# A hybrid decoder trunk on one core: the order of the first loads, the queue of the depthwise taps, and VectorE's convolution chunks in halves of tokens

## The chip, the core and the metric

The program runs on one core of one Trainium2 chip. The core has five engines with a queue of instructions each: TensorE (PE in the profile, its weight loads PEld), VectorE (DVE), ScalarE (ACT), GpSimd (POOL) and SyncE (SP, which here only issues DMAs). An engine runs its own queue strictly in order and waits for semaphores of the others. The metric is the device time of one execution in microseconds. Lower is better.

## What is computed

A two-layer trunk is run on 512 prompt tokens and on 32 sample tokens (8 sequences of 4). Layer 0 is a conformer convolution module, layer 1 stick-breaking attention; each is followed by a convolutional feed-forward block. The change lies in layer 0's first part:

```python
def conformer_conv(h, past, w_in, b_in, w_dw, b_dw, ln_g, ln_b, w_out, b_out):
    u = h @ w_in + b_in                      # h = rms_norm(x); 1024 -> 2048
    a, gate = jnp.split(u, 2, axis=-1)
    glu = a * jax.nn.sigmoid(gate)
    ext = jnp.concatenate([past, glu], axis=1)
    y = causal_dwconv(ext, w_dw, b_dw)       # 31 taps in each of 1024 channels
    y = jax.nn.silu(layer_norm(y, ln_g, ln_b))
    return y @ w_out + b_out, ext[:, -(CONV_WIDTH - 1):]
```

Everything is float32 in and out.

## The kernel before

**Layout and products.** Activations lie transposed: 128 channels on the partitions, eight chunks of channels, 544 tokens along the row (512 of the prompt, then 32). The tokens are worked in two halves, SA (256 tokens) and SB (256 and the 32 samples, so 288). A float32 product is made from three matmuls of a rounded high part and a rest: weights come as `raw` tiles (1 MB, two column chunks of 128, two buffers); ACT casts each column chunk to `whi` (L327), DVE takes the rest `wlo` (L330); such a pair is a slot, and five are kept. In the same way the activations lie as XH and XL. One product of a slot with one token half is 24 matmuls (L650 to L652) into one of four `acc` banks of PSUM.

**The start** (L579 to L619). SP's queue issues, in this order: `mrow` (norm gains), the first two x blocks, the first two weight tiles in column halves (`Ring.load`, L293), the other x blocks and the sample tokens `xs`, eight small loads for `trow` (the first half of the tap rows for TensorE's chunks), two `scr` loads (the convolution's state). GpSimd's queue issues the biases into `mrow`, the seven loads of `prow` (taps and other parameters as rows), some memsets, and the other half of `trow`. Source order and issue order differ for `scr` and `trow`: the profile has `scr` first.

**A list made ahead** (class `Plan`, L77). All work of layer 0 is entered as operations with an engine, an assumed duration, and what they read and write. `run` (L156) plays this list through and fixes each engine's order for PE, DVE, ACT and POOL: it takes the operation that can start first, less a small bonus for the length of what hangs on it, less `urgent`. On the chip each engine then keeps this order whatever the real durations are. `ARRIVE` (L58) holds the assumed times at which loads land. SP's queue is not part of this order; a load goes out when what its buffer waits for is done and what is ahead in the queue has been issued.

**Operations around the change.**
- `WARM` (L915): matmuls without use that keep TensorE busy before data arrive.
- `incoming(h)` (L868): x is transposed on TensorE (L878, into banks `tr` and `av`), ACT scales it to XH (L885), DVE makes XL (L887), one of both copies xT (L891, L893); ACT squares (L896), and from these `rstd` is made (L900 to L912) as a row for all partitions, by a matmul with `dg` (L909).
- `conv_in` (L923): products of four slots with one half; `glu` (L678) evacuates them: `va` (L687) and `sg` (L683) on DVE, both multiplied by `rstd`, the sigmoid on ACT (L685), the product into `ext_p` (L689).
- The depthwise convolution: chunks 2 to 7 go to TensorE (`conv_tensor`, L767) by 32 x 32 diagonal tap matrices `wdg`, which GpSimd makes from `tapc` and `eye` (L763), from copies `rep` of the rows, shifted by a round trip through memory (`shifted`, L739). Chunks 0 and 1 go to DVE (`conv_vector`, L720): for each, one ACT operation for the first tap and 30 SCALAR_TENSOR_TENSOR of 512 columns (L729, L732), accumulating in `dwa`.
- `param_cols` (L855) turns `mrow` and `prow` into columns `prm`; `turn_taps` (L936) turns `trow`, from which ACT copies `tapc` (L942).
- `conv_sample` (L702): the same convolution for the sample tokens on DVE (L711, L716, L718).
- `add_sum` (L785) adds the chunks to `ysum` (L793); `layer_norm(0)` begins with a matmul of it (L809), then subtracts the mean on DVE (L817), and so on.

Of the kernel before, what the change touches and what calls it, by code (L numbers as in the profile page):

```python
# [17 lines left out]
P = 128  # L18
# [23 lines left out]
REPB = 4  # L42
X_AFTER = 2
MORE = 3
# [27 lines left out]

BIG = 1.0e17
E_BUFS, S_BUFS, W_BUFS = 3, 2, 3

# [122 lines left out]
def tile_trunk(  # L198
# [84 lines left out]
    class Ring:  # L283
# [9 lines left out]
        def load(self):  # L293
            if self.nraw >= len(raws):
                return
            src, nk = raws[self.nraw]
            t = ring.tile([P, NC, 2 * P], F32, tag="raw", name=f"raw{self.nraw}", bufs=RAW_BUFS)
            if self.nraw < RAW_BUFS:
                for half in range(2):
                    cols = slice(half * P, (half + 1) * P)  # L300
                    nc.sync.dma_start(out=t[:, :nk, cols], in_=src[:, :, cols])
            else:
                nc.sync.dma_start(out=t[:, :nk, :], in_=src)
            self.raw[self.nraw] = t
            self.nraw += 1

        def prep(self, later=None):
# [60 lines left out]
    def pcol(row, c):  # L368
        return prm[:, c, row:row + 1]
# [18 lines left out]
    def uid(s):  # L388
        _n[0] += 1
        return f"{s}_{_n[0]}"  # L390
# [9 lines left out]
    def act_table(name):  # L400
        tc.keep_in_program_order(act.preload_act_table_set(name))
# [208 lines left out]
    pool.memset(ext_p[:, :, PAST + SEQ:], 0.0)  # L610
    for i, q in enumerate((nc.sync, pool)):
        ch0 = (PE_CHUNKS[0] + i * len(PE_CHUNKS) // 2) * P
        for m in range(8):
            nj = min(4, CW - 4 * m)
            q.dma_start(out=trow[i][m * n_g:(m + 1) * n_g, :nj * 32].rearrange("g (j h) -> g j h", j=nj),
                        in_=conv_w_dw[0, 4 * m:4 * m + nj, ch0:ch0 + n_g * 32].rearrange("j (g h) -> g j h", h=32))
    scf = state_conv.rearrange("o b t d -> (o b t) d")
    for i in range(2):
        nc.sync.dma_start(out=scr[i], in_=scf[i * 120:(i + 1) * 120, :])  # L619

# [41 lines left out]
    def prepare(slot, begin, place):  # L662

        low = []
        raw = slot // 2
        plan.op("act", 0.95, lambda: begin(low), r=[("raw", slot)], w=[*place, ("slot", slot), "prep"])
        plan.op("dve", 1.135, lambda: low[0](), r=[("raw", slot)], w=[("slot", slot), "low"])
        if slot % 2:
            plan.op(f"raw{raw}", 4.5, lambda: None, w=[("raw", slot + 2 * RAW_BUFS + i) for i in (-1, 0)], r=[("slot", slot)])

# [3 lines left out]
    def ext(c, *parts):  # L674

        return [("ext", c, i) for i in parts or range(4)]
# [42 lines left out]

    def conv_vector(c):  # L720

        acc = buf("ctmp", "dwa", [P, SEQ], 2)
        for k in range(CW):
            src = ext_p[:, c, k:k + SEQ]
            if k == 0:
                plan.op("act", 0.6, lambda src=src: act.activation(
                    acc(), src, AF.Identity, scale=pcol(0, c), bias=pcol(R_BDW, c)), r=[*ext(c), "prm"], w=[acc])
            elif k < CW - 1:
                plan.op("dve", 0.61, lambda k=k, src=src: dve.scalar_tensor_tensor(  # L729
                    acc(), src, pcol(k, c), acc(), op0=ALU.mult, op1=ALU.add), r=[*ext(c), "prm"], w=[acc])  # L730
            else:
                plan.op("dve", 0.61, lambda k=k, src=src: dve.scalar_tensor_tensor(  # L732
                    yc[:, c, 0:SEQ], src, pcol(k, c), acc(), op0=ALU.mult, op1=ALU.add),
                    r=[acc, "prm"], w=[("y", c, 0), ("y", c, 1)] + ext(c))

# [118 lines left out]

    def param_cols(rows_t, n, col, r, w):  # L855
# [6 lines left out]
        plan.op("pe", 0.85, turn, r=[r], w=[pt], urgent=URGENT)  # L862
# [3 lines left out]
    param_cols(mrow, 4, R_MIX, "mrow", "mix")  # L866

    def incoming(h):  # L868
# [26 lines left out]
        for t, m, b in mine:  # L895
            plan.op("act", 1.05, lambda t=t, m=m, b=b: act.activation(  # L896
                junk[:m, :D], t, AF.Square, accum_out=ssq[:m, b:b + 1]), r=[("x", b)], w=["junk", ("ss", b)])
        for lo, hi, m in ([(0, 2, P)], [(2, 4, P), (4, 5, NS)])[h]:
# [15 lines left out]

    warm = psum("acc")  # L915
    for i in range(WARM):
        plan.op("pe", 0.1, lambda: pe.transpose(warm()[:, :P], ident, ident), w=[warm])
    incoming(0)
# [16 lines left out]

# [28 lines left out]
    def settle():  # L964
# [1334 lines left out]
```

## Time and profile before

| | us |
|---|---|
| median of 3 runs (lowest, highest) | 1320.45 (1320.37, 1322.04) |
| the profiled execution, its time | 1320.71 |
| its span in the trace | 1319.0 |
| TensorE busy | 1292.6 |
| VectorE busy | 979.0 |
| ScalarE busy | 679.0 |
| GpSimd busy | 161.4 |

A line of a timeline or chain has the start in us, the busy time, the engine, the source line, the operation, output and inputs, the shape and a count; in square brackets stands how long the engine sat idle before it and what ended that. A count above one merges instructions that follow one another; the steps between them are then less than the length of one, because instructions overlap at their ends. A table of stretches gives the busy time of each engine between two times, the mean granted clock of TensorE and the busy share of the DMA engines. Times are from the start of the span.

### The profile page before, as it was taken

How to read it: one execution, taken by the hardware profiler on the slowest of the kernel's cores; microseconds unless marked ns; L12 is line 12 of the kernel's file. 1: busy time of each engine (PE TensorE's matmuls, PEld its weight loads, DVE VectorE, ACT ScalarE, POOL GpSimd, SP SyncE). 2: the span in 40 equal slices, each digit the busy share in tenths (PEclk: the TensorE clock that was granted, in tenths of full speed). 3: DMA queues.
4: the chain of work that ended last, by engine and by line, in shares of the span. 5: the costliest groups of instructions: out<-in, count | busy, mean ns of one | idle time of the engine just before them, and what ended most of it. 6: DMA issues, size and time to landing. Idle time of an engine off the chain costs nothing. (4 is left out here: it accounts for less than half of the span.)

```text
span 1319.0 us, 26810 instructions
## 1 busy us (share of the span) xinstructions
PE 1292.6 (98%) x11066; PEld 1229.5 (93%) x11066; DVE 979.0 (74%) x1651; ACT 679.0 (51%) x1242; POOL 161.4 (12%) x291
## 2 busy tenths in 40 slices
PE   8999999999999999999999999999999999999997
PEld 7997789999999999999999877789999999999996
DVE  4599786788996886868334588875997996886863
ACT  5521385545554454445323688863655555454452
POOL 3200014111010010000122113210011010010000
PEclk9899999999999999999999999999999999999998
DMA  8263443022333233144456224431223233233221
GB/s 233 65 168 116 113 129 99 30 90 88 97 114 112 65 114 113 57 138 146 163 170 191 92 83 137 129 125 65 80 66 112 97 114 110 67 113 97 73 74 68
DMA packets 124492, 142.40 MB, mean 108 GB/s; under 512 B 5672, under 2 KB 117992, under 8 KB 124099
## 3 DMA queue, kind: packets, MB, share of 16 engines
q1 hardware_dynamic: 118003, 122.43, 29.3%
q0 software_dynamic: 6080, 18.25, 4.5%
q8 instruction: 87, 1.43, 0.5%
q14 instruction: 34, 0.28, 0.1%
q10 hardware_dynamic: 288, 0.02, 0.0%
HBM read 129.34 MB, written 12.18 MB: 107 GB/s over the span
## 5 line engine op out<-in xcount | busy, mean ns | idle before, releaser
L327 ACT CAST whi<-raw 128x1024 fp32r<-128x1024 f32 (+2 forms) x244 | 223.1, 917 | 164.1 <-PE tr L1251 31.6
L330 DVE TENSOR_TENSOR wlo<-raw,whi 128x1024 fp32r<-128x1024 f32 (+2 forms) x244 | 256.3, 1055 | 67.1 <-ACT whi L327 66.6
L650 PE MATMUL acc<-XH,whi 128*128 128x288 f32 (+1 forms) x384 | 115.9, 302 | 0.0
L652 PE MATMUL acc<-XH,wlo 128*128 128x288 f32 (+1 forms) x384 | 112.4, 293 | 1.8 <-DVE wlo L330 1.8
L651 PE MATMUL acc<-XL,whi 128*128 128x288 f32 (+1 forms) x384 | 112.5, 293 | 0.0
L414 PE MATMUL acc<-XH,whi 128*128 128x288 f32 (+1 forms) x360 | 107.8, 299 | 1.1 <-DVE xT L2254 1.1
L416 PE MATMUL acc<-XH,wlo 128*128 128x288 f32 (+1 forms) x360 | 103.9, 289 | 0.5 <-DVE wlo L330 0.5
L415 PE MATMUL acc<-XL,whi 128*128 128x288 f32 (+1 forms) x360 | 104.0, 289 | 0.0
L1450 PE MATMUL acc<-TH,whi 128*128 128x272 f32 x288 | 82.9, 288 | 0.0
L1452 PE MATMUL acc<-TH,wlo 128*128 128x272 f32 x288 | 82.9, 288 | 0.0
L1451 PE MATMUL acc<-TL,whi 128*128 128x272 f32 x288 | 82.8, 287 | 0.0
L1486 ACT COPY G<-acc 128x272 f32<-128x272 f32 (+1 forms) x72 | 26.8, 373 | 105.3 <-PE acc L1452 90.5
L650 PEld LDWEIGHTS acc<-XH,whi 128*128 128x128 f32 x384 | 73.7, 192 | 2.7 <-issue 2.1
L652 PEld LDWEIGHTS acc<-XH,wlo 128*128 128x128 f32 x384 | 74.0, 193 | 2.2 <-DVE wlo L330 2.2
L1251 PE MATMUL av<-HL,whi 128*128 128x288 f32 (+1 forms) x256 | 74.6, 291 | 0.3 <-DVE HL L1504 0.3
L1252 PE MATMUL av<-HH,wlo 128*128 128x288 f32 (+1 forms) x256 | 74.1, 289 | 0.7 <-DVE wlo L330 0.7
L1250 PE MATMUL av<-HH,whi 128*128 128x288 f32 (+1 forms) x256 | 74.5, 291 | 0.0
L651 PEld LDWEIGHTS acc<-XL,whi 128*128 128x128 f32 x384 | 73.9, 192 | 0.5
L1250 PE MATMUL tr<-HH,whi 128*128 128x256 f32 (+1 forms) x256 | 73.4, 287 | 0.0
L1251 PE MATMUL tr<-HL,whi 128*128 128x256 f32 (+1 forms) x256 | 73.3, 286 | 0.0
L1252 PE MATMUL tr<-HH,wlo 128*128 128x256 f32 (+1 forms) x256 | 73.0, 285 | 0.0
L414 PEld LDWEIGHTS acc<-XH,whi 128*128 128x128 f32 x360 | 67.8, 188 | 3.9 <-issue 2.4
(395 smaller groups left out, 4307.3 us busy)
## 6 DMA issues: line engine op xcount, KB each, us to landing
raw<-in_ffn_w_gate_dram SPq DMA_DIRECT2D x22, 1024.0 KB
raw<-in_ffn_w_up_dram SPq DMA_DIRECT2D x22, 1024.0 KB
raw<-in_ffn_w_down_dram SPq DMA_DIRECT2D x24, 768.0 KB
raw<-in_attn_w_qkv_dram SPq DMA_DIRECT2D x12, 1024.0 KB
raw<-in_conv_w_in_dram SPq DMA_DIRECT2D x6, 1024.0 KB
rep<-glu SPq DMA_DIRECT2D x36, 142.0 KB
raw<-in_conv_w_out_dram SPq DMA_DIRECT2D x4, 1024.0 KB
raw<-in_ffn_w_down_dram SPq DMA_DIRECT2D x8, 512.0 KB
```

The lines of the kernel that those rows point to most:

```text
L327: act.copy(hi[:, :n, :], src)
L330: dve.tensor_tensor(lo[:, :n, :], src, hi[:, :n, :], op=ALU.subtract)
L414: pe.matmul(o, hi[:, k, :], xh[:, k, c0:c0 + n], start=(k == 0), stop=False)
L415: pe.matmul(o, hi[:, k, :], xl[:, k, c0:c0 + n], start=False, stop=False)
L416: pe.matmul(o, lo[:, k, :], xh[:, k, c0:c0 + n], start=False, stop=(k == nk - 1))
L650: pe.matmul(o, hi[:, k, :], XH[:, k, c0:c0 + n], start=(k == 0), stop=False)
L651: pe.matmul(o, hi[:, k, :], XL[:, k, c0:c0 + n], start=False, stop=False)
L652: pe.matmul(o, lo[:, k, :], XH[:, k, c0:c0 + n], start=False, stop=(k == NC - 1))
L1250: pe.matmul(o, hi[:, j + k, :], xh, start=(start and k == 0), stop=False, **kw)
L1251: pe.matmul(o, hi[:, j + k, :], xl, start=False, stop=False, **kw)
L1252: pe.matmul(o, lo[:, j + k, :], xh, start=False, stop=(stop and k == len(xs) - 1), **kw)
L1450: pe.matmul(o, hi[:, j + k, :], xh, start=(start and k == 0), stop=False, **kw)
```

## The change

Six things are altered, all in layer 0's beginning:

1. SP issues the first loads in another order: `mrow`, x blocks 0 and 1, the two halves of the first weight tile, the first half of the second, x blocks 2 and 3, the second half, the sample tokens. The biases go out on ACT's queue.
2. All 16 `trow` loads go out on GpSimd's queue. The `scr` loads are entered in the list, behind slot 3.
3. The warm matmuls are bf16, 256 columns of a zeroed tile, 45 instead of 40, and do not wait for `ident`.
4. The squares of the first two x blocks are on DVE instead of ACT; the columns of `prow` are made before `incoming(1)` is entered.
5. DVE's chunks 0 and 1 are convolved in halves of 256 tokens: 120 SCALAR_TENSOR_TENSOR of 256 columns and four ACT operations, instead of 60 of 512 and two. The first halves are entered behind `conv_in(0, 0)`, with `dwa` in another pool, so that they need not wait for the start's buffers to be freed.
6. The assumed landing times, the raw tiles' 4.5 to 5.1, and the tap's assumed 0.61 to 0.345 for half the columns.

```diff
-WARM = 40
+WARM = (17, 28)
+WARM_URGENT = 2.5
...
-ARRIVE = {"mrow": 3.2, ("x", 0): 4.4, ("x", 1): 5.9, ("raw", 0): 7.3, ("raw", 1): 8.8, ("raw", 2): 10.3, ("raw", 3): 11.9,
-          ("x", 2): 13.5, ("x", 3): 15.0, ("x", 4): 15.4, "prow": 18.0, "trow": 24.0, "scr": 19.0}
+ARRIVE = {"zero": 1.2, "mrow": 4.8, ("x", 0): 5.0, ("x", 1): 6.6, ("raw", 0): 9.0, ("raw", 1): 10.8, ("raw", 2): 12.6,
+          "prow": 12.0, ("x", 2): 14.4, ("x", 3): 16.2, ("raw", 3): 18.0, ("x", 4): 18.4, "trow": 20.0}
...
+VTAP = 0.345
...
+        def half(self, i):
+
+            src, nk = raws[self.nraw]
+            if not i:
+                self.raw[self.nraw] = ring.tile([P, NC, 2 * P], F32, tag="raw", name=f"raw{self.nraw}", bufs=RAW_BUFS)
+            cols = slice(i * P, (i + 1) * P)
+            nc.sync.dma_start(out=self.raw[self.nraw][:, :nk, cols], in_=src[:, :, cols])
+            self.nraw += i
...
+    zero = conv.tile([P, 2 * P], BF16, name="zero")
+    dve.memset(zero, 0.0)
+    act.dma_start(out=mrow[2:4, :], in_=conv_b_in.rearrange("o (t d) -> (o t) d", t=2))
     act_table("sqrt_and_others")
     nc.sync.dma_start(out=mrow[0:2, :], in_=norm_mix)
     for b in range(2):
         nc.sync.dma_start(out=xr[b], in_=x_prompt[0, b * P:(b + 1) * P, :])
-    for _ in range(X_AFTER):
-        W.load()
+    for i in (0, 1, 0):
+        W.half(i)
     for b in range(2, 4):
         nc.sync.dma_start(out=xr[b], in_=x_prompt[0, b * P:(b + 1) * P, :])
+    W.half(1)
     nc.sync.dma_start(out=xs, in_=x_sample.flatten_outer_dims())
-    for _ in range(RAW_BUFS - X_AFTER):
-        W.load()
-    pool.dma_start(out=mrow[2:4, :], in_=conv_b_in.rearrange("o (t d) -> (o t) d", t=2))
...
-    for i, q in enumerate((nc.sync, pool)):
+    for i in range(2):
...
-            q.dma_start(out=trow[i][m * n_g:(m + 1) * n_g, :nj * 32].rearrange("g (j h) -> g j h", j=nj),
+            pool.dma_start(out=trow[i][m * n_g:(m + 1) * n_g, :nj * 32].rearrange("g (j h) -> g j h", j=nj),
...
-    def conv_vector(c):
+    def conv_vector(c, h):
-        acc = buf("ctmp", "dwa", [P, SEQ], 2)
+        acc = buf(conv, "dwa", [P, 256], 2)
+        lo = 256 * h
+        keys = ext(c, 1, 2, 3) if h else ext(c, 0, 1)
         for k in range(CW):
-            src = ext_p[:, c, k:k + SEQ]
+            src = ext_p[:, c, lo + k:lo + k + 256]
...
+    plan.op("sp", 11.0, states, r=[("slot", 3)], w=["scr"])
...
+            else:
+                plan.op("dve", 1.2, lambda t=t, m=m, b=b: dve.scalar_tensor_tensor(
+                    junk[:m, :D], t, 1.0, t, op0=ALU.mult, op1=ALU.mult, accum_out=ssq[:m, b:b + 1]),
+                    r=[("x", b)], w=["junk", ("ss", b)])
...
+        pe.matmul(warm[0][:, :2 * P], zero[:, :P], zero, start=True, stop=True)
...
+    param_cols(prow, R_MIX, 0, "prow", "prm")
     incoming(1)
     table("sigmoid_and_others")
-    param_cols(prow, R_MIX, 0, "prow", "prm")
...
     conv_in(0, 0)
+    for c in (0, 1):
+        conv_vector(c, 0)
     late["op"] = plan.op("none", 0.0, settle, w=["mrow", "prow", "trow", "scr"] +
                          [(k, b) for b in range(5) for k in ("x", "ss", "dg")])
     conv_in(0, 1)
     for c in (0, 1):
-        conv_vector(c)
+        conv_vector(c, 1)
         conv_sample(c)
```

More of the change, by code (lines that the diff above doesn't have):

```diff
@@ L42 @@
 REPB = 4
-X_AFTER = 2
 MORE = 3
@@ L297, in load @@
             t = ring.tile([P, NC, 2 * P], F32, tag="raw", name=f"raw{self.nraw}", bufs=RAW_BUFS)
[L298 to L303, printed above, removed]
+            nc.sync.dma_start(out=t[:, :nk, :], in_=src)
             self.raw[self.nraw] = t
             self.nraw += 1
+        def half(self, i):
[5 more added lines that the diff above has]
+            self.nraw += i
         def prep(self, later=None):
@@ L614, in tile_trunk @@
             nj = min(4, CW - 4 * m)
[L615 to L619, printed above, removed]
+            pool.dma_start(out=trow[i][m * n_g:(m + 1) * n_g, :nj * 32].rearrange("g (j h) -> g j h", j=nj),
+                          in_=conv_w_dw[0, 4 * m:4 * m + nj, ch0:ch0 + n_g * 32].rearrange("j (g h) -> g j h", h=32))
     plan = Plan(E_CONV)
@@ L668, in prepare @@
         if slot % 2:
-            plan.op(f"raw{raw}", 4.5, lambda: None, w=[("raw", slot + 2 * RAW_BUFS + i) for i in (-1, 0)], r=[("slot", slot)])
+            plan.op(f"raw{raw}", 5.1, lambda: None, w=[("raw", slot + 2 * RAW_BUFS + i) for i in (-1, 0)], r=[("slot", slot)])
     def arrival(key, t):
@@ L718, in conv_sample @@
         plan.op("dve", 0.1, lambda: dve.tensor_scalar(y, y, pcol(R_BDW, c), None, op0=ALU.add), w=[("y", c, 2)])
-    def conv_vector(c):
-        acc = buf("ctmp", "dwa", [P, SEQ], 2)
+    def conv_vector(c, h):
+        acc = buf(conv, "dwa", [P, 256], 2)
+        lo = 256 * h
+        keys = ext(c, 1, 2, 3) if h else ext(c, 0, 1)
         for k in range(CW):
-            src = ext_p[:, c, k:k + SEQ]
+            src = ext_p[:, c, lo + k:lo + k + 256]
             if k == 0:
-                plan.op("act", 0.6, lambda src=src: act.activation(
-                    acc(), src, AF.Identity, scale=pcol(0, c), bias=pcol(R_BDW, c)), r=[*ext(c), "prm"], w=[acc])
+                plan.op("act", 0.36, lambda src=src: act.activation(
+                    acc(), src, AF.Identity, scale=pcol(0, c), bias=pcol(R_BDW, c)), r=[*keys, "prm"], w=[acc])
             elif k < CW - 1:
-                plan.op("dve", 0.61, lambda k=k, src=src: dve.scalar_tensor_tensor(
-                    acc(), src, pcol(k, c), acc(), op0=ALU.mult, op1=ALU.add), r=[*ext(c), "prm"], w=[acc])
-            else:
-                plan.op("dve", 0.61, lambda k=k, src=src: dve.scalar_tensor_tensor(
-                    yc[:, c, 0:SEQ], src, pcol(k, c), acc(), op0=ALU.mult, op1=ALU.add),
-                    r=[acc, "prm"], w=[("y", c, 0), ("y", c, 1)] + ext(c))
+                plan.op("dve", VTAP, lambda k=k, src=src: dve.scalar_tensor_tensor(
+                    acc(), src, pcol(k, c), acc(), op0=ALU.mult, op1=ALU.add), r=[*keys, "prm"], w=[acc])
+            else:
+                plan.op("dve", VTAP, lambda k=k, src=src: dve.scalar_tensor_tensor(
+                    yc[:, c, lo:lo + 256], src, pcol(k, c), acc(), op0=ALU.mult, op1=ALU.add),
+                    r=[acc, "prm"], w=[("y", c, h)] + (ext(c, 1, 2, 3) if h else ext(c, 0)))
     RW = 256 + PAST - 2
@@ L853, in tile_trunk, with states, param_cols @@
         prepare(slot, W.prep, [])
-    def param_cols(rows_t, n, col, r, w):
+    def states():
+        scf = state_conv.rearrange("o b t d -> (o b t) d")
+        for i in range(2):
+            nc.sync.dma_start(out=scr[i], in_=scf[i * 120:(i + 1) * 120, :])
+    plan.op("sp", 11.0, states, r=[("slot", 3)], w=["scr"])
+    def param_cols(rows_t, n, col, r, w, urgent=URGENT):
         pt = psum("tr")
@@ L860, in turn @@
                 pe.transpose(pt()[:, c * n:(c + 1) * n], rows_t[:, c * P:(c + 1) * P], ident[:n, :n])
-        plan.op("pe", 0.85, turn, r=[r], w=[pt], urgent=URGENT)
+        plan.op("pe", 0.85, turn, r=[r], w=[pt], urgent=urgent)
         plan.op("act", 0.1 + 8 * n * 0.9e-3, lambda: act.copy(
             prm[:, :, col:col + n], pt()[:, :NC * n].rearrange("p (c t) -> p c t", c=NC)), r=[pt], w=[w])
-    param_cols(mrow, 4, R_MIX, "mrow", "mix")
+    param_cols(mrow, 4, R_MIX, "mrow", "mix", 0.0)
     def incoming(h):
@@ L895, in incoming @@
         for t, m, b in mine:
[L896 to L897 removed]
+            if h:
+                plan.op("act", 1.05, lambda t=t, m=m, b=b: act.activation(
+                    junk[:m, :D], t, AF.Square, accum_out=ssq[:m, b:b + 1]), r=[("x", b)], w=["junk", ("ss", b)])
+            else:
+                plan.op("dve", 1.2, lambda t=t, m=m, b=b: dve.scalar_tensor_tensor(
+                    junk[:m, :D], t, 1.0, t, op0=ALU.mult, op1=ALU.mult, accum_out=ssq[:m, b:b + 1]),
+                    r=[("x", b)], w=["junk", ("ss", b)])
         for lo, hi, m in ([(0, 2, P)], [(2, 4, P), (4, 5, NS)])[h]:
@@ L912, in incoming, with idle @@
         plan.op("dve", 0.1 + n * 1.05e-3, lambda: dve.tensor_copy(rstd[:, c0:c0 + n], pt()[:, :n]), r=[pt], w=[("R", h)])
-    warm = psum("acc")
-    for i in range(WARM):
-        plan.op("pe", 0.1, lambda: pe.transpose(warm()[:, :P], ident, ident), w=[warm])
+    warm = []
+    def idle():
+        if not warm:
+            warm.append(bank("acc", uid("warm")))
+        pe.matmul(warm[0][:, :2 * P], zero[:, :P], zero, start=True, stop=True)
+    for i in range(sum(WARM)):
+        plan.op("pe", 0.213 if i < WARM[0] else 0.118, idle, r=["zero"], urgent=WARM_URGENT)
     incoming(0)
```

## The prediction

> **What bounds the kernel now.** I read the busy table first, then a table of stretches of my own choosing, then the timeline of each engine in the first 60 us and around the convolution's end. In the stretch rows the columns are start:end, length, busy time of PE, PEld, DVE, ACT and POOL, granted clock, DMA share and GB/s.
>
> ```profile
> span 1319.0 us, 26810 instructions
> PE 1292.6 (98%) x11066; PEld 1229.5 (93%) x11066; DVE 979.0 (74%) x1651; ACT 679.0 (51%) x1242; POOL 161.4 (12%) x291
> ...
> 13.00:30.70 17.70, 15.93 (x115) 14.90 (x113) 9.37 (x18) 11.13 (x23) 0.23 (x1) 0.90 0.86 246
> 30.70:44.30 13.60, 10.81 (x55) 9.38 (x55) 7.13 (x18) 9.87 (x28) 5.27 (x3) 0.75 0.07 22
> 55.70:111.00 55.30, 55.30 (x478) 53.52 (x477) 53.45 (x93) 17.42 (x33) 0.00 (x0) 1.00 0.54 155
> 111.00:145.60 34.60, 34.24 (x524) 23.26 (x523) 33.38 (x54) 4.34 (x9) 3.83 (x2) 1.00 0.44 111
> ```
>
> TensorE bounds the program: from 55.7 us on it hardly stops, so a shift of its work there moves the end. Two places matter. Up to 44.3 us it is short of data and its clock is low (0.90, 0.75). From 55.7 to 145.6 us VectorE is as full as TensorE (53.45 of 55.30, 33.38 of 34.60), and the layer norm's first matmul had to wait for it:
>
> ```profile
> 55.76 0.28 PE L650 MATMUL acc<-XH,whi 128*128 128x256 f32 x1
> ...
> 145.63 0.70 PE L809 MATMUL tr<-ysum,mean_m 128*128 128x256 f32 x2 [0.39 <-DVE ysum L793]
> ...
> 13.21 10.49 SPq L615 DMA_DIRECT2D trow<-in_conv_w_dw_dram  x8
> 23.81 1.02 SPq L303 DMA_DIRECT2D raw<-in_conv_w_in_dram  x2
> ...
> 29.36 1.05 ACT L327 CAST whi<-raw 128x1024 fp32r<-128x1024 f32 x1 [5.59 <-DMA raw<-in_conv_w_in_dram]
> ```
>
> The lower rows show what the first stretch lacks: SP issued the eight tap rows for 10.49 us, the third weight tile went out only at 23.81 and was read at 29.36.
>
> **The change, part by part: the start.** The eight `trow` issues leave SP for GpSimd's queue. POOL has nothing to run before 39.03 (below), so eight more issues there cost nothing if they land before the taps are transposed, near 30 us; if not, DVE waits as long as they are late. The changed SP list has, ahead of the third tile, the same loads and the two `scr` loads, about 5.3 MB; DMA was full for this to about 21 us:
>
> ```profile
> 15.00:20.00 5.00, 3.70 (x19) 3.56 (x18) 4.65 (x10) 4.08 (x10) 0.00 (x0) 0.66 1.00 279
> 20.00:25.00 5.00, 5.00 (x45) 5.00 (x43) 2.60 (x5) 3.71 (x8) 0.00 (x0) 0.99 0.44 102
> ```
>
> so raw2 lands some 3 us later, at 24 instead of 29.36. That is the gain. The half of raw1 that now goes behind x2 and x3 lands near 17; TensorE wants it at 23. The bias row's issue on ACT precedes a table load in an ACT idle to 7 us: nothing. The two squares that move to DVE (some 1.2 us each, by the 1.18 of L711 below) replace ACT work and end by 7.4, before DVE's first PSUM copy. The 45 warm matmuls (bf16, not in this trace; between 0.11 and 0.22 us each, the transposes' steps, warm and cold) replace 40; the first 16 fill the wait for `mrow`, the last 27 the wait for the first weight half.
>
> ```profile
> 147.09 0.29 PE L651 MATMUL acc<-XL,whi 128*128 128x288 f32 x1
> 147.22 0.29 PE L652 MATMUL acc<-XH,wlo 128*128 128x288 f32 x1
> ...
> 176.38 0.28 PE L650 MATMUL acc<-XH,whi 128*128 128x256 f32 x1
> 176.50 0.28 PE L651 MATMUL acc<-XL,whi 128*128 128x256 f32 x1
> ```
>
> A product's matmul takes 0.12 to 0.13 us from start to start. My walk of the changed lists: the first product cannot run on before wlo0, at 12.1. From there to the fifth slot's product (which began at 55.76 above) TensorE has 96 matmuls of 256 columns at 0.118 (11.3), 96 of 288 at 0.133 (12.8), and the transposes and small matmuls, some 6.1: 30.2 us, plus about 1.7 of waits for banks: TensorE gets there at 44 to 45. On its own that is 10 to 11 us early.
>
> But that product needs an accumulator bank that DVE frees only behind `rstd` of the second token half (53.06 and 53.55 below). DVE's new list has 24 of the new half taps and one wlo ahead of it. They start when ACT is through with its chain behind raw2; paces are start to start:
>
> ```profile
> 30.32 0.50 ACT L885 ACTIVATE XH<-av,prm 128x288 fp32r<-128x288 f32 x1
> 30.71 0.49 ACT L885 ACTIVATE XH<-tr,prm 128x288 fp32r<-128x288 f32 x1
> 31.09 0.40 ACT L891 COPY xT<-av 128x288 f32<-128x288 f32 x1
> 31.37 0.42 ACT L891 COPY xT<-tr 128x288 f32<-128x288 f32 x1
> ...
> 34.20 1.28 ACT L401 ACT_TABLE_LOAD   x1
> ...
> 37.14 0.87 DVE L689 SCALAR_TENSOR_TENSOR ext_p<-va,prm,sg 128x256 f32<-128x256 f32 x2
> ...
> 53.06 0.45 DVE L912 COPY rstd<-tr 128x288 f32<-128x288 f32 x1
> 53.55 0.82 DVE L687 TENSOR_TENSOR va<-acc,rstd 128x288 f32<-128x288 f32 x2
> ```
>
> 24 + 0.96 (cast) + 1.36 (two scalings at 0.39, two copies at 0.28) + 0.24 + 1.28 (table) + 0.8 (two sigmoids) + 1.4 (two more scalings, two copies) + 0.4 (first tap, on ACT) = 30.5. A half tap is a 256-column SCALAR_TENSOR_TENSOR: 0.87 for two, so 0.40 a step, where the list is made with 0.345. 24 taps are 9.6, two XL 0.8, a wlo 1.1, small waits 0.5, rstd 0.4: 43.0 at its end, in time for 44.8.
>
> **What stands in the way.** The four `wdg` of GpSimd wait for the taps' transposes, which now come at 32.7, in the middle of these taps. Before, they ran at 39.03 while DVE had nearly nothing. Two later ones met DVE:
>
> ```profile
> 39.03 7.54 POOL L763 TENSOR_TENSOR wdg<-eye,tapc 128x1024 f32<-128x1024 f32 x4 [25.80 <-ACT tapc L942]
> 123.98 1.92 POOL L763 TENSOR_TENSOR wdg<-eye,tapc 128x1024 f32<-128x1024 f32 x1 [77.42 <-PE av L777]
> 130.62 1.91 POOL L763 TENSOR_TENSOR wdg<-eye,tapc 128x1024 f32<-128x1024 f32 x1 [4.72 <-PE av L777]
> ...
> 123.74 1.19 DVE L716 TENSOR_REDUCE ext_p<-prod 128x32 f32<-128x992 f32 x1
> 124.85 2.10 DVE L711 TENSOR_TENSOR prod<-ext_s,prm 128x992 f32<-128x992 f32 x1
> ...
> 128.20 1.18 DVE L711 TENSOR_TENSOR prod<-ext_s,prm 128x992 f32<-128x992 f32 x1
> ...
> 130.73 2.09 DVE L689 SCALAR_TENSOR_TENSOR ext_p<-va,prm,sg 128x256 f32<-128x256 f32 x1
> ...
> 207.21 5.15 POOL L1122 TENSOR_TENSOR u<-xT,rstd 128x256 f32<-128x256 f32 x6 [5.97 <-DVE rstd L1118]
> ...
> 211.67 0.96 DVE L1126 SCALAR_TENSOR_TENSOR XL<-u,prm,XH 128x256 fp32r<-128x256 f32 x1
> ```
>
> A product of two SBUF tiles took 2.10 instead of 1.18, a glu 2.09 instead of some 0.44: each ended one own length after POOL's, so it did not begin before POOL was through. The reduction, with one input, kept its 1.19. At 207 to 212 us POOL's six and DVE's took turns, one each. A tap has two SBUF inputs. Hence four turns of 1.9 + 0.15 with one tap of 0.4 inside each: DVE loses 4 × 1.65 = 6.6 us; its rstd ends at 49.6, the first bank is free at 50.0, and TensorE, there at 44.8, stands for 5.4 us. Bounds: 0 (all gaps) to 7.6 (no tap gets in). The start's gain is 55.76 - 50.2 = 5.5, not 10 to 11.
>
> The Trainium skill says the same of the mechanism (SBUF — State Buffer, Who interferes with whom): a VectorE instruction with two SBUF inputs contends with a GpSimd instruction that reads SBUF, the port pair is locked for the whole instruction, and a reduction never contends. The three DVE rows above agree. It speaks against this change.
>
> A stall this long also costs clock:
>
> ```profile
> 16.44 0.42 PE L652 MATMUL acc<-XH,wlo 128*128 128x256 f32 x1 [1.30 <-DVE wlo L330]
> ...
> 16.50:20.00 3.50, 3.50 (x17) 3.50 (x18) 3.15 (x8) 2.58 (x8) 0.00 (x0) 0.52 0.99 236
> ...
> 33.80:44.20 10.40, 9.06 (x46) 8.12 (x45) 4.12 (x12) 7.09 (x21) 5.17 (x3) 0.68 0.01 2
> ```
>
> After 1.30 us of waiting the clock was 0.52 for 3.5 us (loss 1.7), after the next stop low for 10.4 (up to 5). TensorE is fully fed after these stalls as in the first case, so I take 2 (1.7 to 5). Net start: 3.5 early.
>
> The Trainium skill (TensorE: Matmul & The Clock Gate, What's actually happening) puts a full-rate return behind one busy window of about 3.4 us with a free-running phase; by it a stall costs an estimated 1.7 to 3.4 here.
>
> **VectorE's chunks in halves.** 60 taps of 512 become 120 of 256:
>
> ```profile
> 111.22 0.42 DVE L687 TENSOR_TENSOR va<-acc,rstd 128x256 f32<-128x256 f32 x1
> ...
> 114.53 4.06 DVE L729 SCALAR_TENSOR_TENSOR dwa<-ext_p,prm,dwa 128x512 f32<-128x512 f32 x6
> ```
>
> A full tap's step is (4.06 - 0.75) / 5 = 0.66; two halves are 0.80. The 60 cost 39.8, the 120 47.8: 8.0 us more. 24 of them (9.6) go into DVE's idle time near 31 to 50. The rest is where the list puts it: DVE runs in order, and between two evacuations it gets few taps and then waits for TensorE, so the early ones buy waiting. Behind the `va` at 111.22 the old list has 12 taps (8.0 us) before the layer norm's sum, the new one 41 halves (16.4), and two sums of 0.35 fewer: +7.7. The two late wdg blocked 0.9 and 1.6; now both fall on taps: 3.5, +1.0. About 1.0 of waits for TensorE goes. Old: 111.22 to 145.5, 34.3 us; new: 34.3 + 7.7 + 1.0 - 1.0 = 42. The `va` moves with TensorE by s, the net early start: sum ready at 153 - s less some 0.5 (the old va was itself late by that), 152.5 - s, where TensorE wants it at 145.2 - s. It stands some 7 us. With s = 3.5: 149.0 instead of 145.63, 3.4 late; clock again 2.
>
> **Sum.** +3.4 + 2.0 = +5.4 us. Behind the layer norm lists and work are as before, nothing is given back. The profiled execution took 1320.71 for its 1319.0 span, 0.26 above the median of three (1320.45). 1320.71 + 5.4 = 1326.1; I say **1326**.
>
> **The rivals.**
> - *Both DVE charges fail to bite* (taps slip between the wdg, the tail's taps fill waits): 10.5 early at the fifth slot, carried through less 0.5: 1310.5. For it: the first stretch's loss is real, 13.6 us at a clock of 0.75. Against: the 2.10 and 2.09. It ends on the other side; its point is whether DVE's rstd copy ends before 44.8.
> - *Only the tail bites* (wdg harmless): s = 10.5, sum at 142.0, 3.6 early, clock 2: 1319.
> - *Only the wdg bite*, the tail is absorbed: s = 3.5: 1317. Against: old DVE had 0.39 to spare on the wrong side.
> - *The loads do not come earlier* (raw2 still lands near 29, behind scr), or a cold first stretch: rstd 3 to 5 us later still, s near 0: 1329 to 1332.
>
> **How the numbers follow.** Forecast 0.50, then 0.13, 0.14, 0.12, 0.11 in that order. The range 1313 to 1333 takes in all but the first rival and the far ends of the clock's price. Faster by over 0.2% (2.6 us, about what a measurement of this kernel tells from no change): 0.13 + most of 0.12 = 0.23. Within: 0.14 and the forecast's low edge, 0.17. Slower: 0.60.
>
> **What would show it.** In the changed profile: SP issues raw2 near 14 and ACT casts it near 24; the four wdg lie within 32 to 42 with DVE taps of over 2 us beside them; TensorE waits 4 to 7 us for DVE before the fifth slot's product, then runs at half clock; the first mean matmul begins near 149 after 6 to 8 us of waiting for ysum. Taps of 0.48 throughout, or a mean matmul before 143, would prove me wrong.

## The result, and the profile of the changed kernel

The changed kernel is slower: 1329.26 us in the median of 6 runs (1328.92 to 1331.38), against 1321.29 for the kernel before in the runs beside it (6 runs, 1320.37 to 1322.04). The ratio is 1.0064, 95% interval 1.0051 to 1.0077. The forecast was 1326.

The profiled execution took 1331.38 us with a span of 1329.7, so it lies 2.1 above its own median; against the profiled execution of before (span 1319.0) it is 10.7 longer, and this difference is the one the trace can account for.

From the timeline of the changed kernel, the rows that answer to those of before (start, busy time, engine and line, operation, shape, count; in brackets the idle time ahead and what ended it):

```profile
16.11 0.40 SPq L300 DMA_DIRECT2D raw<-in_conv_w_in_dram  x1
...
28.01 1.05 ACT L333 CAST whi<-raw 128x1024 fp32r<-128x1024 f32 x1 [3.00 <-DMA raw<-in_conv_w_in_dram]
...
36.74 13.66 DVE L736 SCALAR_TENSOR_TENSOR dwa<-ext_p,prm,dwa 128x256 f32<-128x256 f32 x17
...
37.17 8.08 POOL L770 TENSOR_TENSOR wdg<-eye,tapc 128x1024 f32<-128x1024 f32 x4 [18.42 <-ACT tapc L968]
...
53.43 0.45 DVE L932 COPY rstd<-tr 128x288 f32<-128x288 f32 x1
...
54.43 0.58 PE L654 MATMUL acc<-XH,whi 128*128 128x256 f32 x1 [3.48 <-DVE va L691]
...
112.33 0.42 DVE L691 TENSOR_TENSOR va<-acc,rstd 128x256 f32<-128x256 f32 x1 [0.26 <-PE acc L656]
...
154.21 1.22 PE L816 MATMUL tr<-ysum,mean_m 128*128 128x256 f32 x2 [7.43 <-DVE ysum L800]
```

And its table of stretches (start:end, length, busy time of PE, PEld, DVE, ACT, POOL, granted clock, DMA share, GB/s):

```profile
56.00:70.00 14.00, 14.00 (x102) 14.00 (x101) 10.79 (x26) 3.65 (x9) 0.00 (x0) 0.84 0.28 90
70.00:111.00 41.00, 41.00 (x358) 39.22 (x358) 34.99 (x77) 13.17 (x23) 0.00 (x0) 1.00 0.68 178
150.00:180.00 30.00, 24.52 (x244) 20.76 (x248) 21.23 (x48) 14.67 (x29) 0.00 (x0) 0.84 0.29 81
```

Read against before, the account closes in three steps. The fifth slot's product begins at 54.43 instead of 55.76, 1.3 early. From there to the seventh `va` of 256 columns it takes 57.9 us instead of 55.5 (111.22 - 55.76), 2.4 more, while the granted clock is 0.84 up to 70 us: 1.1 late at the `va`. From that `va` to the first mean matmul it takes 41.9 us instead of 34.4, of which TensorE stands 7.43: 8.6 late. Behind it the clock falls once more (0.84 from 150 to 180 us), and the end is 10.7 late. Some 0.9 us of this belong to this one execution: the sixth kernel below comes out as the same program, and every row of its TensorE lies about 0.9 earlier from 10 us on.

### The profile page after: what moved, and what is told of

Same layout as the page of the kernel before. It is cut to its first block, busy times and chain, and to the rows that moved or that the text cites. A ratio compares the mean times of both kernels' runs of the same rounds, so it can differ in the third digit from the quotient of the medians.

```text
span 1329.7 us, 26880 instructions
## 1 busy us (share of the span) xinstructions
PE 1295.8 (97%) x11071; PEld 1231.6 (93%) x11071; DVE 997.6 (75%) x1716; ACT 677.2 (51%) x1240; POOL 164.5 (12%) x298
```

## The experiments

**Theory.** The loads by themselves gain. The half taps lose twice: ahead of the `rstd` copy, where the four `wdg` of GpSimd block them one for one, and behind the `va`, where the list leaves 41 of them. **Rivals:** the loads gain nothing (or harm); the lock is hidden and DVE is late for other reasons; the tail's added work is absorbed. Each experiment was timed against the kernel before on the same chip; ratios are to it. The kernel before's own median moved between 1320.84 and 1322.20 us over these rounds, so a difference between two experiments' medians is good to about 1.4 us. Three numbers of each trace say most: the start of the fifth slot's product (before 55.76, changed 54.43), that of the first mean matmul (145.63, 154.21), and the wait ahead of it (0.39, 7.43).

### One part alone: loads without halves, halves without loads

The first kernel is the changed one with `conv_vector` and its calls as before (full taps of 512 columns):

```diff
-    for c in (0, 1):
-        conv_vector(c, 0)
...
-        conv_vector(c, 1)
+        conv_vector(c)
```

> The changed kernel with its new loads, queues, warm matmuls and squares, but VectorE's chunks in full taps of 512 columns, entered where the kernel before has them. Theory (the halves cost, the loads gain): no tap lies ahead of the rstd copy, so GpSimd's four wdg meet no tap; TensorE runs straight into the fifth slot's product near 50.7 us (the changed kernel stood 3.48 us there and began it at 54.43), some 5 us ahead of the kernel before's 55.76. Behind the va (13 full taps, 12 before) DVE needs 34.4 + 0.7 us, so TensorE waits about 1 us for ysum and the first mean matmul is near 141.5. Time 1316 (1313 to 1318). Rival (the new loads gain nothing, the third weight tile still is read at 28 us): the fifth slot's product at 55 and 1319 to 1321. Rival (the loads themselves cost): over 1323.

Measured: 1314.90 us, ratio 0.9953 (0.9936 to 0.9970). The timeline of TensorE:

```profile
48.45 0.28 PE L654 MATMUL acc<-XH,whi 128*128 128x256 f32 x1
...
138.01 0.70 PE L813 MATMUL tr<-ysum,mean_m 128*128 128x256 f32 x2
```

TensorE runs into the fifth slot's product without a wait, 7.3 us earlier than in the kernel before, and keeps it: the mean matmul is 7.6 earlier. So the loads gain, and what was lost came with the halves. Both marks came 2 to 3.5 us earlier than the expected 50.7 and 141.5. The third weight tile was cast at 27.27 here, so even this gain was not that of a tile that lands at 24.

The second kernel is the one before with the halves alone, the same edit the other way.

> The kernel before with its own loads, and only VectorE's chunks in half taps, entered as in the changed kernel. In the list so made no half tap lies ahead of the rstd copy, and 58 of the 120 lie behind the va at which the kernel before has 12 full taps left (the changed kernel has 41). Theory (the tail of half taps costs, whatever the loads do): start unchanged, fifth slot near 55.8; behind the va 58 x 0.40 = 23.2 instead of 8.0, less three sums of 288 columns, two of 256, one sample product and its sum and one wlo that lie ahead of it or behind the mean here (about 5.5): +9.7; two late wdg on taps +1; TensorE waits some 10 us for ysum, the first mean matmul near 155.5, clock +2: 1331 to 1333. Rival (the wdg's lock, not the tail, is what costs): no taps at the four wdg, hence 1320 to 1322.

Measured: 1331.33 us, ratio 1.0068 (1.0051 to 1.0086). Timeline:

```profile
55.89 0.28 PE L651 MATMUL acc<-XH,whi 128*128 128x256 f32 x1
...
111.03 0.42 DVE L688 TENSOR_TENSOR va<-acc,rstd 128x256 f32<-128x256 f32 x1
...
153.70 1.22 PE L813 MATMUL tr<-ysum,mean_m 128*128 128x256 f32 x2 [8.34 <-DVE ysum L797]
```

The start is that of before, and the tail behind the `va` is 42.7 instead of 34.4 us with 8.34 of standing. No tap lay beside the four `wdg`, so this loss is the tail's (the two late `wdg` in it). The standing was 1.7 short of the 10 expected; the time came out as expected.

### The lock of the four wdg

In the changed kernel four of the 17 taps at 36.74 were slow. Short stretches of its timeline show them apart:

```profile
37.26 2.10 DVE L736 SCALAR_TENSOR_TENSOR dwa<-ext_p,prm,dwa 128x256 f32<-128x256 f32 x1
...
39.28 2.13 DVE L736 SCALAR_TENSOR_TENSOR dwa<-ext_p,prm,dwa 128x256 f32<-128x256 f32 x1
...
41.45 2.02 DVE L736 SCALAR_TENSOR_TENSOR dwa<-ext_p,prm,dwa 128x256 f32<-128x256 f32 x1
...
43.51 2.02 DVE L736 SCALAR_TENSOR_TENSOR dwa<-ext_p,prm,dwa 128x256 f32<-128x256 f32 x1
```

One slow tap goes to each `wdg`, and each is 1.6 to 1.7 longer than a tap's 0.40 to 0.48. That is the pattern; three experiments asked whether it costs time. The first moved the `wdg` forward by entering the transposes of the tap rows ahead of the second half's:

```diff
+    ptt = psum("av")
...
+    plan.op("pe", 0.3, turn_taps, r=["trow"], w=[ptt], urgent=URGENT)
...
+    for c in PE_CHUNKS[:WDG_BUFS]:
+        diagonal(c)
     incoming(1)
     table("sigmoid_and_others")
-    ptt = psum("av")
...
-          "prow": 12.0, ("x", 2): 14.4, ("x", 3): 16.2, ("raw", 3): 18.0, ("x", 4): 18.4, "trow": 20.0}
+          "prow": 12.0, ("x", 2): 14.4, ("x", 3): 16.2, ("raw", 3): 18.0, ("x", 4): 18.4, "trow": 25.0}
```

> The changed kernel with the transposes of the tap rows (and so the four wdg) entered ahead of the second token half's transposes, assumed landing 25 instead of 20. All else stays, halves and loads too. Theory (the lock costs the start, the tail costs the end): the wdg run from about 27 to 35, where DVE waits for the third weight tile; at most one or two of the taps (or wlo, glu) are stretched to 2 us; rstd is through by 49 instead of 53.9, TensorE does not stand ahead of the fifth slot's product (3.48 before) and begins it near 51; with no low clock behind it the va comes 5 us earlier; the tail has 42 half taps and stays 42 us long, with 7 to 8 us of waiting for ysum. Time 1325 to 1326. Rival (the lock is hidden, TensorE is late there for the third weight tile alone): no change from the changed kernel, 1329 to 1331.

Measured: 1328.64 us, ratio 1.0052 (1.0034 to 1.0069): not what the theory gave. The timeline:

```profile
31.37 7.95 POOL L770 TENSOR_TENSOR wdg<-eye,tapc 128x1024 f32<-128x1024 f32 x4 [11.55 <-ACT tapc L966]
31.50 0.69 PE L893 MATMUL av<-ident,xr 128*128 128x128 f32 x2 [3.24 <-ACT tapc L966]
...
54.20 0.28 PE L654 MATMUL acc<-XH,whi 128*128 128x256 f32 x1
```

The `wdg` came at 31.37, not 27, still beside some taps. TensorE's wait ahead of the fifth slot is gone, but it now stands 3.24 us at 28 to 31 for the bank that ScalarE's copy of `tapc` gives back. One wait took the place of another; the run doesn't settle the lock.

The second experiment asked for a wait in the list only:

```diff
-            op=ALU.mult), r=["tapc", "eye"], w=[w])
+            op=ALU.mult), r=["tapc", "eye", ("R", 1)], w=[w])
```

> The changed kernel with GpSimd's first four wdg made to wait for the rstd copy of the second token half; the order of every other engine is the same, 24 half taps still lie ahead of that copy. TensorE first uses a wdg at 99 us. Theory (the four wdg cost DVE 4 x 1.65 us there, and that is TensorE's stall): no tap is over 0.5 us before the copy, which comes at 47 instead of 53.43; TensorE runs into the fifth slot's product at about 50.8 without waiting (54.43 after 3.48 us of waiting) and at full clock; the wdg now stretch wlo, glu products and taps between 47 and 56, which DVE gives back from the 8 us that it waits in 56 to 111. The tail of 41 half taps and its wait for ysum (7.4 us) stay. Some 5.5 us less than the changed kernel: 1323 to 1325. Rival (DVE is late there for its 24 half taps and the third weight tile, lock or no lock): a stall of over 2 us stays, 1328 to 1330. Second rival (the lock only moves and stalls TensorE at the sixth slot): 1327 to 1329.

Measured: 1330.33 us, ratio 1.0066 (1.0052 to 1.0080). The `wdg` ran at 36.31 as before, since nothing they read comes from the `rstd` copy: the list fixes the order on each engine, and a wait on the chip comes only from data or a buffer. So this was the changed kernel once more, and says only how a repeat differs: 0.1% in the median, and in the trace the tile cast at 27.18 instead of 28.01, the fifth slot's product at 53.58 instead of 54.43, after the same 3.5 us of standing. The third gave the wait real data:

```diff
+        if c == PE_CHUNKS[0]:
+            plan.op("pool", 0.1, lambda: pool.tensor_copy(w()[:, 0, 0:1], ext_p[:, 2, PAST:PAST + 1]), r=[("ext", 2, 0)], w=[w])
...
     conv_in(2, 0)
+    for c in PE_CHUNKS[:WDG_BUFS]:
+        diagonal(c)
```

> The changed kernel with GpSimd's first four wdg held by real data: a GpSimd copy of one column of chunk 2's first gated product (made near 62 us) goes into the first wdg ahead of it. (The sixth experiment asked for the wait only in the list, and the wdg ran at 36.31 as ever.) The order of VectorE, TensorE and ScalarE is the same to the instruction; TensorE needs the first wdg at 99 us. Theory (the four wdg cost DVE 4 x 1.65 us ahead of the rstd copy, and that is TensorE's stall): no half tap over 0.5 us before the copy, which comes at 46.8 instead of 53.43; TensorE begins the fifth slot's product at 50.8 (54.43) without waiting and stays at full clock; the wdg now stretch DVE near 62 to 72, which is hidden in the 8.1 us that DVE waited between 56 and 111. The va comes 5 us earlier (112.33), the tail of 41 half taps and its 7.4 us of waiting stay: 1323.5 to 1325.5. Rival (24 half taps and the third weight tile alone make DVE late there): a stall of over 2 us stays, 1328 to 1330. Second rival (the lock only moves): TensorE waits for a bank near 62 to 75, 1326 to 1329.

Measured: 1324.88 us, ratio 1.0024 (1.0015 to 1.0033), 4.4 below the changed kernel. Timeline:

```profile
35.77 7.32 DVE L736 SCALAR_TENSOR_TENSOR dwa<-ext_p,prm,dwa 128x256 f32<-128x256 f32 x17
...
46.58 0.46 DVE L934 COPY rstd<-tr 128x288 f32<-128x288 f32 x1 [0.36 <-PE tr L931]
...
49.77 0.28 PE L654 MATMUL acc<-XH,whi 128*128 128x256 f32 x1
...
62.77 2.14 DVE L693 SCALAR_TENSOR_TENSOR ext_p<-va,prm,sg 128x256 f32<-128x256 f32 x1
...
147.07 1.22 PE L818 MATMUL tr<-ysum,mean_m 128*128 128x256 f32 x2 [7.82 <-DVE ysum L802]
```

The same 17 taps in the same order take 7.32 instead of 13.66 us: the lock cost 6.3. The `rstd` copy is 6.9 earlier (some 1.0 of it lay there before the taps, as in the sixth kernel), TensorE's 3.48 us of standing is gone, and the clock from 56 to 70 us is 1.00. The slow operations are at 62 us now (a glu of 2.14), where DVE had waits to spend. The rival that a stall stays falls, and so does the one that it only moves. The tail's wait stays, 7.82.

### The third weight tile

The fourth kernel holds the two state loads until the fourth slot's rest is made, by data again:

```diff
+    def behind():
+        for i in range(2):
+            pool.tensor_copy(scr[i][:, 0:1], W.w[3][1][:120, 0, 0:1].bitcast(F32))
+
-    plan.op("sp", 11.0, states, r=[("slot", 3)], w=["scr"])
+    plan.op("pool", 0.3, behind, r=[("slot", 3)], w=["scr"])
+    plan.op("sp", 8.0, states, w=["scr"])
```

> The changed kernel with the two state loads (scr, 0.96 MB) held back until the fourth slot's rest is made, so that they stand behind both next weight tiles in SP's queue; a GpSimd copy of one column, which the loads overwrite, makes them wait. Theory (the third weight tile was read at 28.01 and not at 24 since scr stood ahead of it and the fourth tile, issued near 24, shared the DMA engines): it is cast near 23 to 24, the taps start 4 us earlier, the lock by the wdg stays (4 taps of 2 us), 17 taps instead of 24 ahead of rstd; the fifth slot's product at 47 (54.43), the tail has 45 half taps and still some 42 us. Time 1322 to 1325. Rival (the DMA engines are full until 28 us whatever the order, or TensorE's own work bounds the stretch): 1329 to 1331.

Measured: 1326.27 us, ratio 1.0035 (1.0022 to 1.0047), 3.0 below the changed kernel. First its timeline, then one stretch of its table and, last, that stretch of the changed kernel with its neighbours:

```profile
24.02 1.05 ACT L333 CAST whi<-raw 128x1024 fp32r<-128x1024 f32 x1
...
50.37 0.39 PE L654 MATMUL acc<-XH,whi 128*128 128x256 f32 x1 [4.32 <-DVE va L691]
...
149.17 1.22 PE L816 MATMUL tr<-ysum,mean_m 128*128 128x256 f32 x2 [7.60 <-DVE ysum L800]
```

```profile
20.00:24.00 4.00, 4.00 (x35) 3.79 (x34) 3.39 (x8) 3.42 (x7) 0.30 (x2) 1.00 0.31 87
```

```profile
15.00:20.00 5.00, 5.00 (x46) 4.82 (x45) 4.37 (x8) 4.93 (x10) 2.73 (x6) 1.00 1.13 246
20.00:24.00 4.00, 4.00 (x35) 3.79 (x34) 2.80 (x7) 3.31 (x8) 0.00 (x0) 1.00 1.04 224
24.00:28.00 4.00, 4.00 (x35) 3.79 (x34) 1.01 (x3) 0.80 (x2) 0.00 (x0) 1.00 1.06 336
```

The tile is cast at 24.02 without a wait for DMA, and the DMA engines are at 0.31 between 20 and 24 us where they were at 1.04: without the 0.96 MB of state ahead of it the tile is there before ScalarE asks. One trace of each could mislead by a microsecond, but the others agree: the seven kernels that issue the state ahead of the tile and have the new order of loads cast it at 26.79 to 28.01, the four that hold the state back at 23.82 to 24.74. The lock is still there, and with it 4.32 us of standing: TensorE was at the fifth slot by 46.05, close to the 44 to 45 of the prediction. The time missed the expected 1322 to 1325 by 1.3: the copy of `rstd` came at 49.37, so the standing was longer than thought.

The eighth kernel is the one before with only the `trow` issues moved, `enumerate((pool, pool))` in place of `enumerate((nc.sync, pool))`.

> The kernel before with one edit: the eight tap-row loads of SP's queue go out on GpSimd's queue too. The order of every engine and the list stay. Theory (SP's 10.49 us of issuing held the third weight tile back): it is issued when its buffer is free, near 15 to 17 instead of 23.81, and cast near 26 to 27 instead of 29.36, since scr, the other tile and the tap rows share the DMA engines with it; all that hangs on it moves by as much: 1317 to 1319. Rival (the landing is set by the DMA engines' total of 7.7 MB, full until 28 us): 1320 to 1322.

Measured: 1319.83 us, ratio 0.9992 (0.9983 to 1.0001): no change that can be told. The tile is issued at 15.04 instead of 23.81, and cast at 27.56 instead of 29.36. Nine microseconds of issue bought 1.8 of landing and 0.6 at the fifth slot (55.14). The time lies between the theory and the rival; for the rival speaks that the DMA engines stayed full from 15 to 28 us (busy share 1.06). The Trainium skill (DMA: Bandwidth & Descriptors, Issuing engines are not separate DMA queues) says that loads issued by different engines run on the same DMA engines, and only the issuing time is saved; the 1.8 agrees.

The eleventh goes back to the old warm matmuls and to squares on ScalarE, on the first experiment's kernel.

> The first experiment (new loads, full taps) with the warm matmuls of the kernel before (40 transposes of the identity, which wait for GpSimd's identity) and the first two squares on ScalarE as before. Theory (the prediction costed both at nothing): same as the first experiment, 1313 to 1316, fifth slot near 48.5. Rival (the old warm matmuls start 1.3 us later and hold TensorE from the first transposes, and the squares hold ScalarE's first XH): the fifth slot 1 to 3 us later, 1316 to 1318.

Measured: 1315.59 us, ratio 0.9958 (0.9944 to 0.9972), the first experiment's time within its interval, though the fifth slot's product is at 49.97, 1.5 later. The warm matmuls and the squares bring at most those 1.5 us.

### Where the list leaves the half taps

The seventh kernel only tells the list `VTAP = 0.25` instead of 0.345.

> The changed kernel, only with the list told that a half tap takes 0.25 us instead of 0.345 (it takes 0.40 to 0.41). The work is the same; the list puts 32 instead of 24 half taps ahead of the rstd copy, and 25 instead of 41 behind the va. Theory (the end is late for where the list leaves taps, not for the 8 us of work as such): 8 taps more ahead of the copy, 3.2 us more stall before the fifth slot's product (6.7); the tail is 16 x 0.41 = 6.5 shorter, 35.4 instead of 41.9 us, so the wait for ysum goes from 7.4 to some 1 us, and the low clock behind it (2 us) goes. Mean matmul near 151 (154.21), time 1324 to 1327. Rival (the 8 us of added DVE work must be paid somewhere before the mean): TensorE waits elsewhere between 56 and 146 for as much, and the time stays at 1328 to 1332.

Measured: 1324.84 us, ratio 1.0029 (1.0019 to 1.0040). TensorE's waits, in the view of waits (what waited, for whom, us in total, times, longest):

```profile
PE acc L654 <- DVE va L691: 6.9, 1, 6.9
...
PE tr L816 <- DVE ysum L800: 0.9, 1, 0.9
```

As the theory had it: eight more taps ahead of `rstd` make the first wait 6.9 instead of 3.5, and 16 fewer in the tail make the last one 0.9 instead of 7.4. The list's number for a tap, further from the truth, gives an order that is better by 4.4 us.

### All repairs together, with halves and without

> Half taps with every cost found so far taken away as far as it goes: the wdg held as in the ninth experiment, the state loads behind the weight tiles as in the fourth, the list told 0.25 us for a half tap as in the seventh. 22 half taps lie ahead of the rstd copy, 30 behind the va (41 in the changed kernel, 12 full ones in the kernel before). Theory (halves lose by where they stand and by their 8 us, not by being early): the copy is at 44 to 45, TensorE begins the fifth slot's product at 46 without waiting; tail 41.9 - 11 x 0.41 = 37.4 us against some 35 that TensorE gives it, so 2 to 4 us of waiting for ysum and the mean matmul near 139.5, 4 us behind that of the fifth experiment (135.64): 1313 to 1317, slower than the fifth (1310.8) though its DVE starts earlier. Rival (halves fill the idle time at the start and win once the lock is gone): at or below 1310.8.

Measured: 1321.68 us, ratio 1.0000 (0.9991 to 1.0009). This missed the expected 1313 to 1317 by 5 us; the theory had the wait at the wrong place. Timeline:

```profile
123.08 1.79 DVE L739 SCALAR_TENSOR_TENSOR ext_p<-ext_p,prm,dwa 128x256 f32<-128x256 f32 x1
124.79 0.47 DVE L693 SCALAR_TENSOR_TENSOR ext_p<-va,prm,sg 128x256 f32<-128x256 f32 x1
...
132.67 12.56 PE L786 MATMUL av<-rep,wdg 128*32 128x256 f32 x192 [4.79 <-issue]
...
146.88 0.70 PE L818 MATMUL tr<-ysum,mean_m 128*128 128x256 f32 x2 [0.66 <-DVE ysum L802]
```

TensorE hardly waits for `ysum`, but stands 4.79 us (and 1.73 earlier) at the diagonal matmuls. Behind the half taps the gated product of chunk 6 comes only at 124.79, and its rows go through memory to those matmuls (the store is issued at 125.29, the loads from 127.95 on). That chain is read from the trace and was not tried by itself.

The fifth kernel has the new loads, full taps, and the state loads held back.

> The new loads with full taps of 512 columns (as in the first experiment) and the state loads held behind both next weight tiles (as in the fourth). Theory (each removes its own cost, and they add): the third weight tile is cast near 23.5 instead of 27.27, TensorE reaches the fifth slot's product at 45 to 46 (it was there at 46.05 in the fourth experiment) instead of 48.45, no tap is ahead of rstd, so it need not wait; everything behind is 2.4 to 3 us earlier: 1312 to 1313. Rival (VectorE, busy 40.51 of 41 us between 70 and 111 in the first experiment, becomes the bound): the wait for ysum grows from 0.7 to 3 us and the time stays at 1314 to 1316.

Measured: 1310.80 us, ratio 0.9925 (0.9912 to 0.9939): 10 us faster than the kernel before, 18 faster than the changed one, and 1.2 below what was expected. Timeline:

```profile
37.96 5.38 DVE L336 TENSOR_TENSOR wlo<-raw,whi 128x1024 fp32r<-128x1024 f32 x2 [4.57 <-ACT whi L333]
...
45.78 0.28 PE L654 MATMUL acc<-XH,whi 128*128 128x256 f32 x1
...
135.64 0.70 PE L813 MATMUL tr<-ysum,mean_m 128*128 128x256 f32 x2 [0.38 <-DVE ysum L797]
```

The `wdg` are beside two `wlo` (5.38 us; 1.23 each where nothing is beside them), and nobody waits for them. The twelfth kernel held the `wdg` in this one too, as in the ninth.

> The fifth experiment (new loads, full taps, state loads behind both weight tiles) with the four wdg held as in the ninth; the order of VectorE, TensorE and ScalarE is the same to the instruction. In the fifth, the wdg stretched two wlo (5.38 us for two that take 2.28) ahead of the rstd copy at 43.27, and TensorE reached the fifth slot's product at 45.78 without a wait. Theory (the lock costs only where DVE's result is awaited): the copy comes earlier by at most 3 us and nobody waits for it, so 1310 to 1312, the same within 0.2%; held to near 56 the wdg stretch full taps where DVE is busy 13.68 of 14 us, so if there is an effect it is a loss of 1 to 5 us. Rival (the lock costs wherever it falls): 2 to 3 us faster than the fifth.

Measured: 1315.76 us, ratio 0.9962 (0.9948 to 0.9976), 5 slower than the fifth kernel. Timeline:

```profile
42.51 0.46 DVE L936 COPY rstd<-tr 128x288 f32<-128x288 f32 x1 [1.80 <-PE tr L933]
...
45.70 0.28 PE L654 MATMUL acc<-XH,whi 128*128 128x256 f32 x1
...
61.57 5.39 DVE L733 SCALAR_TENSOR_TENSOR dwa<-ext_p,prm,dwa 128x512 f32<-128x512 f32 x3
...
106.50 0.42 DVE L691 TENSOR_TENSOR va<-acc,rstd 128x256 f32<-128x256 f32 x1
...
118.94 0.49 DVE L693 SCALAR_TENSOR_TENSOR ext_p<-va,prm,sg 128x256 f32<-128x256 f32 x1 [0.30 <-ACT sg L689]
...
119.46 0.34 SPq L750 DMA_DIRECT2D glu<-ext_p  x1
121.69 1.97 SPq L754 DMA_DIRECT2D rep<-glu  x4
...
127.36 11.89 PE L783 MATMUL av<-rep,wdg 128*32 128x256 f32 x192 [3.52 <-issue]
```

The edit that gained 4.4 in the ninth loses 5 here, the far end of what the expectation had allowed. The `rstd` copy is earlier and TensorE is not. Between 57 and 67 us a glu and several full taps are stretched, where DVE has no idle time to make up for it: it is 5.3 late at its `va` at 106.50 (101.24 in the fifth kernel). TensorE is not late yet; its rows lie within 0.3 us of the fifth kernel's up to 123 us. Then it stands 3.52 us at the diagonal matmuls, as in the tenth kernel: the gated product of chunk 6 came at 118.94 (112.07 in the fifth kernel), and its rows went through memory first. With the low clock behind this stop (0.60 from 127.3 to 130.8 us) it is 5.0 late, and the mean matmul comes at 140.60 instead of 135.64. How much of this wait is the chain through memory is read from the trace and was not tried.

## Why the prediction was right in sign and short in size

1. **The third weight tile at 24: wrong, and this is the step that failed.** It was cast at 28.01 (27.18 in the repeat). SP issued it at 16.11, 2 later than said, but that was not the cause: with the state loads out of its way, issued at 15.52, it was there for a cast at 24.02. The working counted the state's bytes ahead of the tile and had all that moved by 21 us, as in the kernel before; then it gave the tile's 1 MB 3 us, some 350 GB/s. In the changed kernel the rate was 246 GB/s from 15 to 20 us and 224 from 20 to 24, and the fourth tile, issued at 23.76, moved beside the rest. How the 4 us divide between the two was not tried. The 4 us went straight through: taps at 34.71 instead of 30.5, `rstd` at its end at 53.9 instead of 49.6, the fifth slot's product at 54.43 instead of 50.2.
2. **TensorE on its own at 44 to 45.** It was there at 50.95 (54.43 less the 3.48; 50.07 in the repeat), and at 46.05 in the fourth kernel, with the tile early. So the tile is most of the difference, and the estimate of TensorE's own work was right to 1 or 2 us.
3. **The lock, 6.6 us: right**, 6.3 measured by the ninth kernel. The stall was 3.48 and not 5.4, since TensorE was late too, by some 6 us where DVE was 4.3 late.
4. **The clock behind the stall, 2: right**, 2.4. So 1.1 late at the `va` where the sum had 3.5 early. Of these 4.6, the tile is 4.2 and the clock 0.4.
5. **The tail, 42 us and some 7 of standing: right**, 41.9 and 7.43. The clock behind it, 2: 2.1. The seventh kernel bears this out: it stood only 0.9 us there, and from its mean matmul to the end it took 1173.1 us where the changed kernel took 1175.5.
6. **The sum**: 5.4 was said, 10.7 is the difference of the profiled executions, and 8.0 that of the medians. The 5.3 between 5.4 and 10.7 are the 4.6 of the start and 0.6 of the tail (7.5 instead of 6.9), and some 0.9 of them are this execution's own. Against the medians the sum was 2.6 short. The range of 1313 to 1333 held gains too, so that the time lay in it says little; the two charges that made the sign are what the experiments bear out.
7. **The costs set at nothing** (warm matmuls, squares, issues on GpSimd's queue) held: the eleventh and eighth kernels are within 0.1% of the first and of the kernel before. The squares ended at 9.5 and not by 7.4, still ahead of DVE's first copy from PSUM at 9.79.
8. **The rivals.** What happened has the forecast's two charges and the fourth rival's start: the tile still lay behind the state loads and landed near 28, so that s was near 0, and the time fell at the foot of that rival's 1329 to 1332. It had 0.11.

## What to carry to other kernels

In these traces GpSimd's products of two SBUF tiles and VectorE's two-input operations took turns: each product of 2.0 us let one tap through, which came out 1.6 to 1.7 us longer. In these kernels that was paid only where VectorE's result was awaited (the changed kernel) or where it had no idle time left (the twelfth), so it is worth knowing what will be beside it after a change, not only before. When a load is moved ahead, count the bytes that remain ahead of it in its queue, at the rate of the stretch in which they will move, and the loads that will move beside it; issuing it earlier moved its landing little here. A tap cut in half cost more in sum (0.66 became 2 x 0.40), and a list that plans with a wrong duration decides where that is paid.

## What the runs showed that was not expected

- Moving the tile's issue from 23.81 to 15.04 moved its cast only from 29.36 to 27.56; taking 0.96 MB from ahead of it moved it from 28.01 (27.18 in the repeat) to 24.02.
- Holding the same four `wdg` to the same later place in the list gained 4.4 us in one kernel and lost 5.0 in another that differs in its taps and first loads.
- In the fifth kernel the granted clock is 1.00 in every stretch from 26 to 180 us, and TensorE's 135.64 at the mean matmul is 10 us ahead of before; those 10 us are also the difference of the times (1320.84 to 1310.80).
